# Weight stores and raw loads on GpSimd's queue, and the bonus' high part on GpSimd

## The chip, the cores and the metric

The kernel runs on one core of one Trainium2 chip. The metric is the time of one execution in device microseconds (us). The engines are named as in the profile: PE (TensorE, matrix products), DVE (VectorE), ACT (ScalarE), POOL (GpSimd) and SP (SyncE, which here only issues DMAs). DMAs can be issued by SP, ACT and POOL; each issue is an instruction in that engine's own stream, and an instruction that has to wait holds up all that stand behind it on its engine.

## The reference

One layer of a diffusion backbone over 128 context and 2048 latent tokens of 1024 channels. What matters here is the first part, up to the operands of the recurrence:

```python
h = _rmsnorm(x, norm_g) * (1 + scale) + shift          # scale, shift from c @ w_ada
proj = h @ w_in                                         # 1024 x 4096
r, k, v, g_a, b_gate, c_gate, u_conv, g_b = split(proj)
r, k, v = token_shift(r, k, v)                          # neighbours in the row
decay, a = low-rank maps of h (tanh / sigmoid), two directions
kk = k * kk_scale;  kk = kk * rsqrt(max(sum(kk * kk over a head), 1e-24))
kd = k * (1 + (a - 1) * ka_scale)                       # per direction
bonus = sum(r * kd * bonus_rk over a head, both directions)
y = groupnorm(scan(r, decay, kd, v, kk, a)) + bonus * v
```

Behind it come the bidirectional scan, the gates, the output projection with w_out, and a final norm.

## The kernel before, in words

All products are made in a split form: a float32 tensor is written as a high part in the matrix engine's format and a low part (the rest), and three products are summed: high by high, high by low, low by high. This holds for the weights and for the normalised input h, and for the small sums over a head, which are products with a matrix of ones.

The program has three phases, built by `phase1`, `phase2` and `phase3`. The change lies in `phase1`, which computes the projection and its followers. Tokens are cut into six blocks (`BLK`, five of 384 and one of 256), and two blocks form a third (`THIRD`). The outer loop runs over the thirds; within one, four groups `g` of 128 channels and two turns each (`turn`) load the weight blocks of 128 output channels that they need and run `mixA`, `gateA`, `convB` and `gateB` over the third's two token blocks.

- `load_w` (lines 117 to 129) gets a weight block. In the first third it is new: the raw block is loaded from `in_win` (line 124, tile `wr`, two buffers), ACT copies it into the high part (line 125), DVE subtracts for the low part (line 126, tile `w`, four buffers), and both parts are stored to the scratch tensor `scr_wsp` (line 127). In the second and third third the split block is loaded back from there (line 121).
- `parts_of` (lines 192 to 198) makes the parts of the summands of a head's sum: the high part `hsh` (line 196), the low part `hsl` (line 197). `part_sum` then runs two products with the ones (lines 204 and 205). It is called with names that begin with s for the squares of kk (`hshs`), with b for the bonus (`hshb`, from the tile `kd` that line 407 writes), and with q for the squares of a token block's norm (`hshq`).
- `shifted` (lines 313 to 330) copies a projection out of PSUM twice on ACT (lines 319 and 321), adds the neighbours on POOL (line 323, reading the padded tile `rawl`, two buffers) and joins both on DVE (line 329).
- `mixA` writes its results into tiles `sp` (four buffers) and spills them with SP (`spill`, line 335) to scratch tensors in memory, `scr_ops` among them; lines 387, 390, 398, 401 and 402 on DVE write these tiles.
- At the start the modulation is computed: `wadas` tiles are loaded (line 249), the rows are multiplied (line 190), copied (line 259), transposed (line 264), and made into scale and shift (lines 270 to 272). `norm_steps` squares a token block on ACT (lines 216 and 219), sums on DVE (line 220), and `make_h` makes h (lines 148 to 150). The first weight blocks, 32 and 33 (`wlora`), then 4 and 0 (`ws0`), are loaded in between, as are the token blocks x0 and x1 (line 177).

The order of the instructions on each engine isn't the order of the program text: a scheduler sets it when the program is built, from an estimate of each operation's duration. Changing one operation's engine can therefore move others.

Of the kernel before, what the change touches and what calls it, by code (L numbers as in the profile page):

```python
# [6 lines left out]
F32 = mybir.dt.float32  # L7
# [42 lines left out]
def phase1(K):  # L50
    nc, tc, A, S = K.nc, K.tc, K.A, K.S
    V, G, P, T = nc.vector, nc.gpsimd, nc.scalar, nc.tensor
# [64 lines left out]
    def load_w(cb):  # L117

        w = wp.tile([128, 2, 8, 128], F32R, tag="w", name=f"w{cb}_{K.u()}", bufs=4)
        if cb in kept:  # L120
            nc.sync.dma_start(w[:].bitcast(F32), S["wsp"][cb])
            return w
        raw = wp.tile([128, 8, 128], F32, tag="wr", name=f"wr{cb}_{K.u()}", bufs=2)
        nc.sync.dma_start(raw[:], A["win"][cb])
        P.copy(w[:, 0], raw[:])
        V.tensor_tensor(w[:, 1], raw[:], w[:, 0].bitcast(F32), ALU.subtract)
        nc.sync.dma_start(S["wsp"][cb], w[:].bitcast(F32))
        kept.add(cb)
        return w

# [61 lines left out]
    def parts_of(t_, n, nm, eng):  # L192

        hi = ta_.tile([128, 384], F32R, tag="hsh", name=f"hsh{nm}", bufs=1)
        lo = ta_.tile([128, 384], F32R, tag="vt", name=f"hsl{nm}", bufs=1)
        P.copy(hi[:, :n], t_[:, :n])  # L196
        eng.tensor_tensor(lo[:, :n], t_[:, :n], hi[:, :n].bitcast(F32), ALU.subtract)  # L197
        return hi, lo

    def part_sum(o, t_, n, nm, eng=G):  # L200

        hi, lo = parts_of(t_, n, nm, eng)
        ps = pax.tile([128, 384], F32, tag="ax", name=f"ps{nm}")
        T.matmul(ps[:, :n], o[:], hi[:, :n], start=True, stop=False)
        T.matmul(ps[:, :n], o[:], lo[:, :n], start=False, stop=True)
        return ps
# [38 lines left out]
    for i, b in enumerate((0, 2, 1, 3)):  # L245
# [7 lines left out]
        if i == 1:  # L253
            wlora = [load_w(32), load_w(33)]
            x1 = load_x(1, ca, "upx")
        if i == 2:
            ws0 = [load_w(cb) for cb in (4, 0)]
# [312 lines left out]

    for t3, js in enumerate(THIRD):
        wd, wi = wlora if t3 == 0 else (load_w(32), load_w(33))
        lws, pre, conv, sums = {}, {}, {}, {}
        more = coming(*THIRD[t3 + 1]) if t3 < 2 else iter(())
# [834 lines left out]
```

## Time and profile before

| | before |
|---|---|
| median of 3 runs | 1766.98 us (1766.21 to 1769.92) |
| profiled execution | 1765.65 us |
| its span, first to last instruction | 1763.5 us |
| mean granted clock of PE | 0.972 |
| DMA queue of SP (q1) | 323.99 MB, 61.5% of 16 engines' span |
| DMA queue of POOL (q0) | 4.46 MB, 0.7% |
| first raw load, last store of line 127 | issued at 7.1 and 358.6 us |
| phase 1's first third | up to about 400 us |

The profile shows one execution; its columns are explained where rows are shown. A line such as L124 is the line of the kernel's text. In the rows that group waits, the numbers are the total in us, the count, and the longest. In rows in order of time, the first number is the start in us, the second the duration, and the brackets hold how long the engine was idle just before and what released it.

### The profile page before, as it was taken

Reading aid. Unit: us, or ns where it says so; the run is one execution under the profiler, and the core shown is the slowest. Engines: PE = TensorE matmul, PEld = TensorE weight load, DVE = VectorE, ACT = ScalarE, POOL = GpSimd, SP = SyncE. Lnnn points to the kernel's source line nnn. Section 1 sums busy time; section 2 is a strip of 40 time slices with the busy share of each in tenths; the row PEclk is TensorE's granted clock in tenths of the full one; section 3 lists DMA queues with packets and bytes.
Section 4 is the critical chain, followed back from the end, with each engine's and each line's share of the span. In section 5 each row is a group of like instructions: output and inputs, shape, how many; then the busy total and the mean of one; then the engine's idle time right before and its main releaser. Section 6 shows DMA issues by size and latency. Waiting matters only on the chain. (4 is left out here: it accounts for less than half of the span.)

```text
span 1763.5 us, 33040 instructions
## 1 busy us (share of the span) xinstructions
PE 1638.5 (93%) x12400; PEld 1544.7 (88%) x12400; DVE 1163.8 (66%) x2249; ACT 815.3 (46%) x1583; POOL 585.4 (33%) x1089
## 2 busy tenths in 40 slices
PE   5999999998999998999999789899799899899998
PEld 2888889898999998999999789899799899887786
DVE  6875788866466866556773666677677777656333
ACT  4533455434144433334342367567577576533222
POOL 0011111101011111011120777767777868323221
PEclk8999999999999999999999899899999999899999
DMA  9787778785456646567767566667766875645442
GB/s 364 208 234 217 232 251 256 227 251 145 151 147 228 171 149 168 173 212 233 222 196 255 135 168 170 151 162 182 187 161 185 187 181 128 180 158 193 152 143 90
DMA packets 315664, 335.15 MB, mean 190 GB/s; under 512 B 166953, under 2 KB 263849, under 8 KB 301425
## 3 DMA queue, kind: packets, MB, share of 16 engines
q1 hardware_dynamic: 243200, 323.99, 61.5%
q10 hardware_dynamic: 70944, 4.60, 2.8%
q0 software_dynamic: 1360, 4.46, 0.7%
q8 instruction: 98, 1.61, 0.4%
q14 instruction: 62, 0.50, 0.1%
HBM read 221.16 MB, written 111.82 MB: 189 GB/s over the span
## 5 line engine op out<-in xcount | busy, mean ns | idle before, releaser
L934 POOL TENSOR_TENSOR zt<-zt,ztmp 128x30 f32<-128x30 f32 (+7 forms) x510 | 199.0, 390 | 39.1
L1010 PE MATMUL psE<-str,stl 128*128 128x128 f32 x1088 | 147.4, 280 | 13.0 <-DVE E L1011 11.1
L1050 PE MATMUL psS<-sv,E 128*128 128x64 f32 x1088 | 154.6, 274 | 2.0 <-DVE sv L1063 1.9
L1050 PEld LDWEIGHTS psS<-sv,E 128*128 128x128 f32 x1088 | 144.5, 198 | 5.2 <-DVE sv L1063 3.0
L1010 PEld LDWEIGHTS psE<-str,stl 128*128 128x128 f32 x1088 | 132.2, 193 | 15.4 <-DVE E L1011 12.0
L931 POOL TENSOR_TENSOR ztmp<-ab,zt 128x60 f32<-128x60 f32 (+7 forms) x255 | 133.1, 522 | 19.3
L779 ACT COPY bd<-rr 64x512 f32<-64x512 f32 x136 | 83.9, 617 | 84.1 <-issue 27.2
L323 POOL TENSOR_TENSOR shk<-rawl 128x384 f32<-128x384 f32 (+1 forms) x24 | 22.1, 920 | 292.3 <-ACT rawl L319 292.3
L1011 DVE TENSOR_TENSOR E<-psE,msk 128x512 f32<-128x512 f32 x136 | 93.2, 686 | 30.2 <-PE psE L1010 28.1
L1063 DVE TENSOR_TENSOR sv<-psS,pc 64x128 f32<-64x128 f32 x254 | 68.0, 277 | 42.1 <-PE psS L1050 40.4
L999 PE MATMUL psX<-F,zb 128*128 128x128 f32 x544 | 77.7, 295 | 18.5 <-DVE E L1011 17.1
L999 PEld LDWEIGHTS psX<-F,zb 128*128 128x128 f32 x544 | 70.5, 206 | 21.6 <-DVE E L1011 20.0
L892 PE MATMUL psF<-rr,bd 128*128 128x128 f32 x544 | 79.0, 291 | 9.9 <-DMA rr<-scr_ops 3.9
L1345 POOL TENSOR_TENSOR z<-z,x 128x512 f32<-128x512 f32 x32 | 43.6, 1366 | 129.1 <-DVE z L1341 107.1
L892 PE MATMUL psG<-rr,bd 128*128 128x128 f32 x544 | 73.9, 282 | 10.1 <-DVE F L893 10.1
L197 POOL TENSOR_TENSOR hslb<-kd,hshb 128x384 fp32r<-128x384 f32 (+1 forms) x24 | 26.0, 1084 | 163.7 <-ACT hshb L196 157.6
L892 PEld LDWEIGHTS psF<-rr,bd 128*128 128x128 f32 x544 | 70.3, 202 | 11.4 <-issue 6.1
L160 PE MATMUL mmc<-h,w 128*128 128x384 f32 (+1 forms) x192 | 67.5, 352 | 13.3 <-ACT q1r L321 9.7
L892 PEld LDWEIGHTS psG<-rr,bd 128*128 128x128 f32 x544 | 67.6, 196 | 10.4 <-DVE F L893 10.3
L323 POOL TENSOR_TENSOR shv<-rawl 128x384 f32<-128x384 f32 (+1 forms) x24 | 21.3, 888 | 151.9 <-ACT rawl L319 146.5
L893 DVE TENSOR_TENSOR F<-psF,msk 128x512 f32<-128x512 f32 x68 | 46.4, 683 | 30.4 <-PE psF L892 16.5
L162 PE MATMUL mmc<-h,w 128*128 128x384 f32 (+1 forms) x192 | 66.0, 344 | 0.0
(307 smaller groups left out, 5230.4 us busy)
## 6 DMA issues: line engine op xcount, KB each, us to landing
w<-scr_wsp SPq DMA_DIRECT2D x68, 1024.0 KB, 7.0
scr_wsp<-w SPq DMA_DIRECT2D x34, 1024.0 KB, 5.9
rr<-scr_ops SPq DMA_DIRECT2D x64, 512.0 KB, 4.8
scr_ops<-sp SPq DMA_DIRECT2D x160, 192.0 KB, 5.3
wr<-in_win SPq DMA_DIRECT2D x34, 512.0 KB, 6.3
ab<-scr_at SPq DMA_DIRECT2D x34, 256.0 KB, 4.1
x<-in_x SPq DMA_DIRECT2D x17, 512.0 KB, 3.8
wadas<-in_wada SPq DMA_DIRECT2D x8, 1024.0 KB, 13.0
```

What stands on the lines that cost most here:

```text
L160: T.matmul(ps[:, :n], w[:, 0, k], hh[:, 0, k, :n], start=k == 0, stop=False)
L162: T.matmul(ps[:, :n], w[:, 1, k], hh[:, 0, k, :n], start=False, stop=k == 7)
L779: (V.tensor_copy if k in ON_DVE else P.copy)(dst, src)
L892: T.matmul(ps[:, i, :].rearrange("p (a b) -> p a b", b=64), w[:, u, :], x[:, :, u, :], start=True, stop=True)
L893: V.tensor_tensor(dst[:, h * 4:h * 4 + 4, :], ps[:], mask.unsqueeze(1).broadcast_to((128, 4, 128)), ALU.mult)
L931: G.tensor_tensor(tv, ab[:, j:j + 2, j + 2:32].unsqueeze(1).broadcast_to((128, kn, 2, n)), zt[:, :kn, j:j + 2].unsqueeze(3).broadcast_to(( ...
L934: G.tensor_tensor(zt[:, :kn, j + 2:32], zt[:, :kn, j + 2:32], tv[:, :, r], ALU.subtract)
L999: T.matmul(px[:, i, :], B.zb[:, gi, us.start + i, :], g.F[:, us.start + i, :], start=True, stop=True)
L1010: T.matmul(pe[:, i, hd, :].rearrange("p (b t) -> p b t", b=2), g.lt[:, :, hd, us.start + k + i].rearrange("p b t -> p (b t)"), g.rt[:, :, ...
L1011: V.tensor_tensor(g.E[n][:, k:k + 2].rearrange("p a b c -> p (a b) c"), pe[:].rearrange("p a b c -> p (a b) c"), B.msk[:, ME[g.d]].unsquee ...
L1050: T.matmul(sp[gi][:, q, hd, :], g.E[n][:, k, hd, :], sv[:, u, hd, :], start=True, stop=True)
L1063: r = V.tensor_tensor(dst, sp[gi][0:64, q], B.pc[0:64, d, 2 * p:2 * p + 2, c:c + 1].broadcast_to((64, 2, 64)), ALU.mult)
```

## The change

Both DMAs of a new weight block, the raw load and the store of the parts, are issued by POOL instead of SP. And the high part of the bonus' summands (names that begin with b) is copied by POOL instead of ACT; the low part was POOL's already. The other sums' high parts stay on ACT. As each of the 34 weight blocks is new once, 34 loads and 34 stores move; 24 copies move, one for each group and token block, in all thirds.

```diff
         raw = wp.tile([128, 8, 128], F32, tag="wr", name=f"wr{cb}_{K.u()}", bufs=2)
-        nc.sync.dma_start(raw[:], A["win"][cb])
+        G.dma_start(raw[:], A["win"][cb])
         P.copy(w[:, 0], raw[:])
         V.tensor_tensor(w[:, 1], raw[:], w[:, 0].bitcast(F32), ALU.subtract)
-        nc.sync.dma_start(S["wsp"][cb], w[:].bitcast(F32))
+        G.dma_start(S["wsp"][cb], w[:].bitcast(F32))
...
         hi = ta_.tile([128, 384], F32R, tag="hsh", name=f"hsh{nm}", bufs=1)
         lo = ta_.tile([128, 384], F32R, tag="vt", name=f"hsl{nm}", bufs=1)
-        P.copy(hi[:, :n], t_[:, :n])
+        (G.tensor_copy if nm[0] == "b" else P.copy)(hi[:, :n], t_[:, :n])
         eng.tensor_tensor(lo[:, :n], t_[:, :n], hi[:, :n].bitcast(F32), ALU.subtract)
```

`G`, `V` and `P` are POOL, DVE and ACT.

## The prediction

> **What bounds the kernel now.** I read the busy times first, then a table of stretches, then the waits of each engine, then single rows in order of time.
>
> ```profile
> span 1763.5 us, 33040 instructions
> ```
>
> ```profile
> PE 1638.5 (93%) x12400; PEld 1544.7 (88%) x12400; DVE 1163.8 (66%) x2249; ACT 815.3 (46%) x1583; POOL 585.4 (33%) x1089
> ```
>
> TensorE (PE) is busy for 1638.5 of 1763.5 us, and only the 125 us that it is idle can be won; what makes it idle more is lost in full. The stretches say where that idle time lies (columns: busy time of PE, weight load, DVE, ACT, POOL, then granted clock, DMA share, GB/s).
>
> ```profile
> core 0: us, PE busy (x) PEld busy (x) DVE busy (x) ACT busy (x) POOL busy (x), PEclk, DMA share, GB/s
> 0.00:20.00 20.00, 7.64 (x40) 1.80 (x40) 6.07 (x23) 7.23 (x13) 1.27 (x15) 0.87 0.89 336
> 20.00:40.00 20.00, 15.50 (x84) 8.88 (x76) 16.62 (x36) 10.73 (x22) 0.00 (x0) 0.70 1.03 416
> 40.00:60.00 20.00, 15.64 (x71) 13.72 (x68) 19.39 (x42) 10.62 (x19) 0.00 (x0) 0.83 0.63 218
> ```
>
> ```profile
> 60.00:400.00 340.00, 321.76 (x1769) 305.29 (x1768) 253.88 (x449) 152.28 (x287) 44.37 (x42) 0.98 0.79 233
> 400.00:720.00 320.00, 304.22 (x1722) 299.76 (x1721) 202.90 (x365) 115.87 (x233) 40.81 (x42) 0.99 0.60 173
> ```
>
> There are three regimes. Up to 40 us the DMA engines are full (share 0.89 and 1.03, 336 and 416 GB/s): the start waits for data. From 40 to 60 us VectorE is full (19.39 of 20): it makes the normalised inputs. From 60 us on PE is the bound, with 340 - 321.76 = 18.2 us idle in the rest of the first third. The moved DMAs all lie before 360 us; the bonus edit reaches on to 910 us. The next rows are the waits in 60 to 400 us that the change touches (total, times, longest).
>
> ```profile
> SPq L127 <- DVE w L126: 72.4, 21, 12.1
> ```
>
> ```profile
> DVE sp L387 <- DMA scr_ops<-sp: 17.2, 6, 4.6
> ```
>
> ```profile
> ACT w L125 <- DMA wr<-in_win: 40.4, 14, 5.1
> ACT hshb L196 <- DVE kd L407: 21.1, 7, 6.3
> ```
>
> SyncE's queue stands for 72.4 us before weight stores whose data VectorE hasn't made. VectorE waits for operand spills, issued by the same queue, to land. ScalarE waits 40.4 us for raw weight blocks.
>
> **The change part by part.** It takes 34 stores of 1024 KB and 34 loads of 512 KB off SyncE's queue and puts them into GpSimd's instruction stream, and it moves 24 copies from ScalarE to GpSimd. In the built order the blocks keep their sequence; the start differs most, so it comes first.
>
> *Start.* Sizes and landings:
>
> ```profile
> scr_wsp<-w SPq DMA_DIRECT2D x34, 1024.0 KB, 5.9
> ```
>
> ```profile
> wr<-in_win SPq DMA_DIRECT2D x34, 512.0 KB, 6.3
> ```
>
> ```profile
> 8.47 0.43 SPq L177 DMA_DIRECT2D x<-in_xt  x1
> ```
>
> ```profile
> 22.89 0.33 SPq L127 DMA_DIRECT2D scr_wsp<-w  x1
> ```
>
> ```profile
> 25.65 0.52 ACT L216 ACTIVATE ssq<-x 128x384 f32<-128x384 f32 x1 [2.19 <-DMA x<-in_xt]
> ```
>
> ```profile
> 29.44 0.55 DVE L220 TENSOR_TENSOR ssq<-ssq,sqx 128x384 f32<-128x384 f32 x1
> ```
>
> ```profile
> 26.81 2.72 DVE L148 SCALAR_TENSOR_TENSOR x<-x,gs,ssq 128x128 f32<-128x128 f32 x8
> ```
>
> Before, one queue gives the order: the first two stores are issued at 22.89 us and later, behind the second input block x1 (issued 8.47 us) and the modulation weights. After, the first two raw loads are GpSimd's first DMAs, ScalarE's casts of them stand ahead of the squares of x0, and VectorE's two subtractions (L126) ahead of the sum of squares. So both stores and the next two raw loads are ready some 10 us after the start and travel beside x0 and x1: 2 x 1024 + 2 x 512 KB = 3.15 MB that weren't ahead of x1 before. At the mean of 336 and 416 GB/s they take 8.4 us. How two queues share the engines no row shows, so x1 lands between 0 and 8.4 us later than 25.65 us; I take the middle, 4.2 us. And the built order makes this bind: ScalarE now has four squares of x1 before the first h (L149), VectorE two of x1's sums before L148. Before, L148 began at 26.81 us, 1.16 us after x1; after, two squares (0.5 us each) and two sums lie between, about 2.0 us: +0.8, of which 1.1 us comes back because two sums of 0.55 us are then already made. With 19.39 of 20 us busy behind it, VectorE can't make the delay good, and at 60 us PE takes it over. Term: **+3.9 us** (ends -0.3 and +8.1). Nothing hides it; if the stores stayed behind x1, it would be nil.
>
> [...]
>
> *SyncE's queue freed.* Spills no longer stand behind the 72.4 us of store waits, nor on the same queue behind 1024 KB. VectorE's 17.2 us for spills shrink. What PE pays for that I take from PE's rows:
>
> ```profile
> 97.56 0.45 PE L365 MATMUL up<-lw,ups 128*128 128x384 f32 x1 [1.93 <-ACT q1r L321]
> 100.26 0.69 PE L160 MATMUL mmc<-h,w 128*128 128x384 f32 x1 [2.08 <-ACT ta L384]
> ```
>
> ```profile
> 159.80 0.44 PE L204 MATMUL pss<-hshs,onr 128*128 128x384 f32 x1 [2.38 <-ACT hshs L196]
> ```
>
> ```profile
> 182.98 0.44 PE L204 MATMUL pss<-hshs,onr 128*128 128x384 f32 x1 [1.77 <-ACT hshs L196]
> ```
>
> ```profile
> 264.56 0.44 PE L365 MATMUL up<-lw,ups 128*128 128x384 f32 x1 [1.30 <-ACT q1r L321]
> ```
>
> Followed back, the one at 182.98 us comes from a spill (1.8 us); the other four, 7.7 us, come from ScalarE standing at a late raw block, which the change doesn't cure: a load still follows its own store. Term: **-1.5 us** (0 to -1.8; the rivals take more).
>
> *GpSimd's stream.* The nearest rows for its DMAs are those of the second phase, a store of a quarter of the size.
>
> ```profile
> L935 POOL DMA_DIRECT2D scr_zt<-zt x17: 582/604/757, 1004.9 to 1519.4; - x17
> ```
>
> ```profile
> scr_zt<-zt POOLq DMA_DIRECT2D x17, 256.0 KB, 3.2
> ```
>
> An issue holds GpSimd for 0.60 us, and 3.2 us to landing is no more than the 5.9 of SyncE's larger stores. 68 x 0.60 = 41 us fit into the 296 us that GpSimd idles in 60 to 400 us. What counts is order: each store waits for VectorE's subtraction, and behind it are queued the shifted sums (VectorE waits for those) and the low parts (PE waits). The times that each operation has now, set against the new order, show what that costs. Of 42 operations one stands behind a DMA that is due later:
>
> ```profile
> 183.00 1.30 POOL L197 TENSOR_TENSOR hsls<-sq,hshs 128x384 fp32r<-128x384 f32 x1 [6.23 <-ACT hshs L196]
> ```
>
> ```profile
> 186.57 0.43 SPq L124 DMA_DIRECT2D wr<-in_win  x1
> ```
>
> That is 3.6 us on one low part. The other way round, six raw loads now stand behind operations that end 0.4 to 2.5 us after the load's present issue, 8.8 us together; the first and the last pair:
>
> ```profile
> 83.99 1.42 POOL L197 TENSOR_TENSOR hsls<-sq,hshs 128x384 fp32r<-128x384 f32 x1 [17.85 <-ACT hshs L196]
> ```
>
> ```profile
> 85.00 0.39 SPq L124 DMA_DIRECT2D wr<-in_win  x1
> ```
>
> ```profile
> 303.32 0.83 POOL L323 TENSOR_TENSOR shv<-rawl 128x384 f32<-128x384 f32 x1
> ```
>
> ```profile
> 302.88 0.42 SPq L124 DMA_DIRECT2D wr<-in_win  x1
> ```
>
> PE paid 7.7 us for ScalarE's 40.4, a fifth; a fifth of 8.8 is 1.7 us. Term: **+1.5 us** (0 to 3.6 + 1.7 = 5.3).
>
> [...]
>
> *The bonus' high part.* ScalarE's copy goes, GpSimd gets one of the same size.
>
> ```profile
> L196 ACT CAST hshb<-kd x24: 406/513/517, 87.0 to 908.0; 128x384 fp32r<-128x384 f32 x20, 128x256 fp32r<-128x256 f32 x4
> ```
>
> ```profile
> L197 POOL TENSOR_TENSOR hslb<-kd,hshb 128x384 fp32r<-128x384 f32 x20 | 23.1, 1153 | 145.5 <-ACT hshb L196 139.3 <-PE pss L205 6.2
> ```
>
> GpSimd's copy isn't in the trace; it has one input where the subtraction has two, so it lies between ScalarE's 0.51 and the subtraction's 1.15 us: 0 to 0.64 us later per sum. ScalarE no longer stands at kd (21.1 us in the first third), but PE waits little for what is behind it. Where PE does wait for this part, kd itself is late, and that stays:
>
> ```profile
> 688.77 0.44 PE L204 MATMUL psb<-hshb,onr 128*128 128x384 f32 x1 [3.25 <-ACT hshb L196]
> ```
>
> Gain at most those 3.25 us; loss at most 24 x 0.64 x a fifth = 3.1 us. Term: **+0.1 us**.
>
> Sum: 3.9 - 1.5 + 1.5 + 0.1 = +4.0 us. Its own ends are -0.3 - 1.8 + 0 - 3.2 = -5.3 and 8.1 + 0 + 5.3 + 3.1 = +16.5. The profiled execution took 1765.65 us (2.15 around its span), 1.3 below the median of 1766.98, so it becomes 1769.7, and a median **1771.0 us**. This case's ends are 1762 and 1783.
>
> **The rivals.** First, faster: the start costs nothing, because the stores come too late to matter or SyncE's transfers hold their share, and freeing the queue wins more than one PE wait, also raw blocks that land sooner. Of the 18.2 us PE idle, the five rows hold 9.5; with two thirds gone, -6.3, so 1760.7 us. For it: 72.4 us of waits leave SyncE. Against: loads keep their place behind stores, and PE is 94% busy there. It decides if x1 lands before about 26 us. Second, no change: the start costs +1.5 and the queue gives it back, 1767 us. Third, slower on a larger scale: each time a raw block is late, GpSimd stands at its store until VectorE's subtraction (1.22 us in the next row) and two issues are done, 2.4 us longer than ScalarE stands. At all 14 late blocks that is 34 us, a fifth of it on PE 6.8; with the start at its upper end, 8.1 + 6.8 = +15, so 1782 us. Against: only one of 42 operations stood behind a later DMA. It decides if low parts wait over 1 us at most stores.
>
> ```profile
> L126 DVE TENSOR_TENSOR w<-wr,w x34: 1162/1219/1641, 21.6 to 357.3; 128x1024 fp32r<-128x1024 f32 x34
> ```
>
> [...] That the edit does nothing is excluded: the built order shows all 68 DMAs and 24 copies moved.
>
> The later phases are also reordered a little on PE; I see no sign in it and count it only in the range.
>
> **How the numbers follow.** Forecast (slower by about 4 us) 0.37, first rival 0.27, second 0.20, third 0.12, fourth 0.04. A measurement of this kernel tells about 0.2%, 3.5 us, from no change. The forecast's case reaches from a little below its bound to +12; of its 0.37 some 0.04 falls inside 0.2%, while the second rival gives 0.03 to either side. Slower 0.33 + 0.16 + 0.03 = 0.52, same 0.04 + 0.14 = 0.18, faster 0.27 + 0.03 = 0.30. The range takes the first rival's figure with a few us below it and the third's: 1758 to 1786 us. The forecast's own range is 1762 to 1783.
>
> **What would show it.** Right: the first square of x1 (L216) some 4 us later than 25.65, L148 near 31, PE's first shifted operands near 68; GpSimd's issues near 0.60 us; VectorE's wait for spills before 400 us well under 17.2; PE's waits for the bonus' parts as before. [...]

## The result and the profile after

The changed kernel takes 1779.21 us in the median of 11 runs (1771.36 to 1785.17); the kernel before, run beside it, takes 1767.36 us (1763.94 to 1769.92). The ratio is 1.0061, 95% interval 1.0043 to 1.0078: slower by 10.8 us (7.6 to 13.8). The profiled execution of the changed kernel took 1784.01 us. Its page begins:

```profile
span 1782.2 us, 33110 instructions
...
PE 1641.3 (92%) x12400; PEld 1548.9 (87%) x12400; DVE 1164.4 (65%) x2249; ACT 804.0 (45%) x1559; POOL 638.6 (36%) x1181
```

PE does the same work (1641.3 us against 1638.5) and idles for 140.9 us where it idled for 125.0. The stretches, columns as before:

```profile
0.00:20.00 20.00, 5.74 (x24) 2.21 (x24) 4.67 (x18) 5.08 (x6) 4.67 (x21) 1.00 0.88 318
20.00:40.00 20.00, 8.59 (x36) 3.59 (x40) 12.26 (x28) 10.23 (x24) 0.00 (x0) 1.00 1.03 419
```

```profile
60.00:400.00 340.00, 316.71 (x1706) 297.62 (x1705) 260.99 (x461) 152.99 (x288) 83.37 (x108) 0.96 0.78 224
```

Up to 40 us the DMA engines are as full as before (318 and 419 GB/s), but PE gets 14.33 us of work done instead of 23.14, and VectorE 16.93 instead of 22.69: the engines carry bytes that nobody waits for yet. From 60 to 400 us PE idles for 23.3 us instead of 18.2. The rows that answer to the predicted first steps, from the order of time on ACT and DVE:

```profile
33.74 0.52 ACT L216 ACTIVATE ssq<-x 128x384 f32<-128x384 f32 x1 [0.90 <-DMA x<-in_xt]
```

```profile
36.58 2.71 DVE L148 SCALAR_TENSOR_TENSOR x<-x,gs,ssq 128x128 f32<-128x128 f32 x8
```

x1's first square is 8.1 us later (25.65 before) and L148 9.8 us later (26.81 before). The waits of 60 to 400 us (total, times, longest):

```profile
POOL scr_wsp L127 <- DVE w L126: 68.2, 14, 10.1
ACT w L125 <- DMA wr<-in_win: 39.0, 14, 6.8
...
POOL hshb L196 <- DVE kd L407: 24.9, 5, 9.2
...
DVE sp L387 <- DMA scr_ops<-sp: 15.2, 4, 5.0
```

The 72.4 us for which SP stood at the stores until VectorE's low part was made are now POOL's 68.2; ScalarE waits for raw blocks as long as before (39.0 against 40.4), and VectorE for spills nearly as long (15.2 against 17.2).

### The profile page after: what moved, and what is told of

The parts are those of the page before. It is cut to its first block, busy times and chain, and to the rows that moved or that the text cites. A ratio compares the mean times of both kernels' runs of the same rounds, so it can differ in the third digit from the quotient of the medians.

```text
span 1782.2 us, 33110 instructions
## 1 busy us (share of the span) xinstructions
PE 1641.3 (92%) x12400; PEld 1548.9 (87%) x12400; DVE 1164.4 (65%) x2249; ACT 804.0 (45%) x1559; POOL 638.6 (36%) x1181
## 5 line engine op out<-in xcount | busy, mean ns | idle before, releaser
L160 PE MATMUL mmc<-h,w 128*128 128x384 f32 (+1 forms) x192 | 68.5, 357 | 16.9 <-ACT q1r L321 14.5
L127 POOL DMA_DIRECT2D scr_wsp<-w x34 | 19.0, 560 | 143.0 <-DVE w L126 83.5
L161 PE MATMUL mmc<-h,w 128*128 128x384 f32 (+1 forms) x192 | 67.0, 349 | 0.0
L162 PE MATMUL mmc<-h,w 128*128 128x384 f32 (+1 forms) x192 | 66.7, 348 | 0.0
```

The costliest lines, as they stand in the source:

```text
L160: T.matmul(ps[:, :n], w[:, 0, k], hh[:, 0, k, :n], start=k == 0, stop=False)
L161: T.matmul(ps[:, :n], w[:, 0, k], hh[:, 1, k, :n], start=False, stop=False)
L162: T.matmul(ps[:, :n], w[:, 1, k], hh[:, 0, k, :n], start=False, stop=k == 7)
```

## The experiments

I held two theories when I began. **Start**: the first four blocks' DMAs take the DMA engines from what the start needs, and that delay stays to the end. **Stream**: from the fifth block on, loads and stores in one stream on GpSimd come late for each other. The rival was **Bonus**, the copy itself, on which the expectations of e3 and e4 put a price of its own.

These runs were made on three chips, on which the kernel before took 1774 to 1775 us in the median, so versions are compared by their ratio to the runs of before beside them. The table also holds two places of each profile: L148, and the start of the first product (`mml`) of the second third, which sums up the first third. In the profiles they read, for before and after:

```profile
390.08 0.33 PE L160 MATMUL mml<-h,w 128*128 128x384 f32 x1
```

```profile
407.28 0.33 PE L160 MATMUL mml<-h,w 128*128 128x384 f32 x1
```

| version | L148 | second third | ratio to before (95%) | us |
|---|---|---|---|---|
| before; again | 26.81; 26.73 | 390.1; 391.5 | 1 | |
| the change; again | 36.58; 36.38 | 407.3; 405.8 | 1.0061 (1.0043 to 1.0078); 1.0068 (1.0042 to 1.0093) | +10.8; +12.1 |
| e1: first four blocks on SP | 26.64 | 403.4 | 1.0053 (1.0034 to 1.0072) | +9.4 |
| e2: first four blocks alone on GpSimd | 36.69 | 407.6 | 1.0107 (1.0079 to 1.0135) | +19.0 |
| e3: all DMAs, no bonus copy | 36.54 | 405.6 | 1.0022 (1.0000 to 1.0045) | +3.9 |
| e4: bonus copy alone | 26.75 | 395.4 | 1.0026 (1.0002 to 1.0050) | +4.6 |
| e7: later stores alone | 26.90 | 393.4 | 0.9991 (0.9971 to 1.0011) | -1.6 |
| e8: later loads alone | 27.05 | 394.4 | 1.0006 (0.9991 to 1.0022) | +1.1 |
| e9: later loads and stores | 26.74 | 397.7 | 1.0059 (1.0037 to 1.0082) | +10.5 |
| e10: first four blocks on ScalarE's queue | 43.77 | 411.7 | 1.0090 (1.0068 to 1.0113) | +16.0 |
| e11: x1 loaded first | 26.78 | 394.5 | 0.9999 (0.9985 to 1.0014) | -0.2 |
| e12: x1 first, later stores | 27.48 | 396.1 | 1.0005 (0.9990 to 1.0021) | +0.9 |

The us are the ratio's distance from 1 times the median of before in the same set of runs (1774.83 for e1 to e4, 1774.03 for e7, e8 and the second run of the change, 1773.91 for e9 to e12).

**e1, e2: the start put back, and the start alone.**

```diff
-        G.dma_start(raw[:], A["win"][cb])
+        (nc.sync if cb in (32, 33, 4, 0) else G).dma_start(raw[:], A["win"][cb])
...
-        G.dma_start(S["wsp"][cb], w[:].bitcast(F32))
+        (nc.sync if cb in (32, 33, 4, 0) else G).dma_start(S["wsp"][cb], w[:].bitcast(F32))
```

That is e1, against the changed kernel. e2 has `G` and `nc.sync` the other way round in both lines, and the bonus' copy on ScalarE.

> The changed kernel, but the first four weight blocks (32, 33, 4, 0) are loaded and stored by SyncE's queue again; the other thirty and the bonus' copy stay with GpSimd. Theory Start (the stores and raw loads of these four travel beside x0, the modulation weights and x1, and the 9.8 us by which the first shift comes later stay to the end): x1's first square near 26 us, the first shift near 27, and the time about 10 us below the changed kernel's 1779, so 1768 to 1771. Theory Stream (GpSimd stands at the later stores and loads, or its adds come behind them; PE loses another 5 us between 60 and 400 us): the start is as before, but the time stays 5 us or more above before's 1767, so 1772 to 1776, and PE is idle for about 23 us between 60 and 400 us as in the changed kernel.

> The kernel before, with the loads and stores of the first four weight blocks alone (32, 33, 4, 0) on GpSimd's queue; everything else on SyncE's and ScalarE's as before. Theory Start: x1's first square near 33 us, the first shift near 36, PE's work from there on 9 to 10 us later, the time about 10 us above before's, 1776 to 1778. Theory Stream: the later blocks are needed for the loss; the start's delay is partly made up before 60 us and the time is 1767 to 1772.

In e1 the start is as before to 0.2 us, and the loss stays: +9.4 us. Start alone is not the cause. In e2 L148 is 9.9 us late, as in the changed kernel, and the whole version is slower by 14 to 24 us. Start is enough to make the kernel slower, and by more than its 10 us; at the second third e2 is as late as the change (407.6 against 407.3 and 405.8).

In e1 PE runs level with before up to 110 us and then falls back by several us, first at one place. In order of time, on GpSimd, ScalarE and PE:

```profile
114.98 0.58 POOL L127 DMA_DIRECT2D scr_wsp<-w  x1 [6.23 <-DVE w L126]
115.56 0.53 POOL L124 DMA_DIRECT2D wr<-in_win  x1
```

```profile
126.83 1.04 ACT L125 CAST w<-wr 128x1024 fp32r<-128x1024 f32 x1 [10.36 <-DMA wr<-in_win]
```

```profile
127.93 0.69 PE L160 MATMUL mmb<-h,w 128*128 128x384 f32 x1 [4.49 <-ACT w L125]
```

The raw load is issued 0.58 us behind a store for which GpSimd stood until VectorE's low part was made, and its 512 KB need 11.3 us to land; the store's 1024 KB, in the same queue ahead, need 10.0. ScalarE idles for 10.36 us, PE for 4.49. Why both take so long comes with e8 and e9.

**e3, e4: the bonus.** e3 puts line 196 back to `P.copy`; e4 is before with the changed line 196 alone.

> The changed kernel with the bonus' high part copied by ScalarE again; all DMAs of the first third's blocks stay with GpSimd. Theories Start and Stream: nothing much changes, 1777 to 1782, within 3 us of the changed kernel. Theory Bonus (GpSimd's copy stands behind a store's wait, or takes GpSimd's time in the later thirds, where the changed kernel's PE falls back by another 6 us between 720 and 1080 us): 4 to 8 us under the changed kernel.

> The kernel before, with the bonus' high part alone copied by GpSimd; all DMAs on SyncE's queue. Theories Start and Stream: within 2 us of before, 1765 to 1769. Theory Bonus: 3 us or more above before, 1770 to 1775.

Both came out as the rival Bonus had it: alone the copy costs 4.6 us (0.4 to 8.9), and with it the DMAs cost 7 us more than without (e3 against the change). Yet by the time of the whole it adds nothing to the later DMAs (e1 against e9), though at the second third e1 is 5.7 us behind e9. The contrasts disagree, and no row here shows what the copy would cost. So Bonus is neither shown nor excluded; nothing to 9 us is what the runs leave.

**Again: two executions of one program.**

> The kernel before, unchanged, for a second profile: how far do two executions of one program differ? If times and places are made by the instructions' order, every stall of over 1 us between 60 and 400 us comes back at its place, x1's first square is near 25.6 us, PE's idle time there is 18 us within 1.5, and the span moves only with the granted clock. If they are chance, stalls of several us come at other places.

> The changed kernel, unchanged, on the same chip and beside the same runs of before as the part kernels. Theory Start (its 10 us stay to the end): about 10 us above before. Theory Start and Stream: the two add up, 15 to 19 us above before. If the two cover each other (blocks that are late wait for nobody when PE is late as well): 5 to 10 us, no more than the start alone or the later blocks alone.

The stalls come back at their places. Before: 2.38 us at 159.80 and 2.20 at 159.01, 1.77 at 182.98 and 2.00 at 182.33. After: 4.21 at 191.88 and 4.78 at 192.14. The change came out at +12.1 us here (7.5 to 16.5), between mere cover (5 to 10) and the full sum (15 to 19), and its interval touches both. Up to 700 us two executions agree to about 3 us. Behind that they part: the first product of phase 2 (`psF`) came at 939.3 us and at 948.6 us in two executions of before. So profiles are read here up to the second third, and ends by the ratios alone.

**e7, e8, e9: later stores, later loads, both.** Each is the kernel before with the first four blocks on SP and the bonus on ScalarE; e7 puts line 127 on `G` from the fifth block on, e8 line 124, e9 both.

> The kernel before, with the stores alone on GpSimd's queue, from the fifth block on; all loads and the first four blocks stay with SyncE. Theory Stream (a raw load stands behind the store of the block before it on GpSimd, which waits for VectorE's low part): no load stands there, so within 2 us of before, or up to 3 us faster since SyncE is freed. If stores on GpSimd hold up its adds: 4 us or more above before, and PE waits for the shifted sums or low parts.

> The kernel before, with the raw loads alone on GpSimd's queue, from the fifth block on; all stores and the first four blocks stay with SyncE. Theory Stream: a load stands no longer behind a store, only behind GpSimd's adds and subtractions, so the wait of 4.5 us near 128 us for the ScalarE copy of a late block is gone and the time is within 3 us of before. If GpSimd's own work is enough to make loads late: that wait is there, 3 us or more, and the time is 5 to 9 us above before.

> The kernel before, with loads and stores of all blocks from the fifth on on GpSimd's queue; the first four blocks stay with SyncE, the bonus' copy with ScalarE. Stores alone and loads alone cost nothing that could be measured, so theory Stream (it takes both, since only then a load stands behind the store of the block before it) says: a wait of 3 to 5 us for the ScalarE copy of a late block near 128 us, PE 7 to 13 us later than before from 130 us on, and a time 5 to 9 us above before. If the loss of the version with the bonus' copy came from that copy: no such wait, and within 3 us of before.

Neither alone costs anything that can be measured; both together cost 10.5 us (6.6 to 14.5). That is Stream, without bonus and without the start, though not quite as I expected it: the time is above the 5 to 9 us, and PE's wait near 128 us is 2.34 us instead of 3 to 5. The same block in e8 and in e9:

```profile
113.25 0.53 POOL L124 DMA_DIRECT2D wr<-in_win  x1 [12.06 <-DVE w L126]
```

```profile
120.71 1.07 ACT L125 CAST w<-wr 128x1024 fp32r<-128x1024 f32 x1
```

```profile
115.24 0.58 POOL L127 DMA_DIRECT2D scr_wsp<-w  x1 [5.02 <-DVE w L126]
115.82 0.53 POOL L124 DMA_DIRECT2D wr<-in_win  x1
```

```profile
125.59 1.04 ACT L125 CAST w<-wr 128x1024 fp32r<-128x1024 f32 x1 [5.72 <-DMA wr<-in_win]
126.69 0.44 PE L160 MATMUL mmb<-h,w 128*128 128x384 f32 x1 [2.34 <-ACT w L125]
```

In e8 (first two fences) the load, too, waits for VectorE, which frees its raw buffer, but no store goes ahead of it in its queue: it lands 6.4 us on, and ScalarE doesn't wait. In e9 it is issued 2.6 us later, behind the store, and lands 9.8 us on.

The store's bytes ahead are only a part of that. Stretches of e9 and then of e8 (DMA share and GB/s are the last two columns):

```profile
116.00:122.00 6.00, 6.00 (x35) 5.66 (x34) 6.00 (x8) 1.43 (x4) 2.62 (x4) 1.00 0.99 135
122.00:128.00 6.00, 2.96 (x16) 2.33 (x14) 2.23 (x5) 2.19 (x4) 0.00 (x0) 1.00 0.94 388
```

```profile
112.00:119.00 7.00, 7.00 (x41) 6.76 (x39) 7.00 (x11) 3.52 (x6) 1.56 (x2) 1.00 0.90 309
120.00:126.00 6.00, 6.00 (x34) 5.91 (x35) 6.00 (x7) 2.81 (x7) 1.90 (x2) 1.00 1.04 111
```

Each has 6 us in which the DMA engines are full by their packets' times and move a third of what they move beside it. In both this follows a small transfer that ScalarE issues, `scr_pc` (line 392): 784 packets, 0.003 MB, which start at 115.3 us in e9 and at 119.4 in e8, and in e1 at 115.1, with 130 GB/s from 116 to 122 us. In e9 and e1 the store and the load fall into this stretch; in e8 the load has landed before it, at 119.6 us. So the late block has two candidates, the store ahead in the queue and the small transfer ahead of both, and no run parts them. This is one place. Another is common to e1, e9, e3 and both profiles of the change; e9's rows, on DVE, ACT and PE:

```profile
184.74 0.56 DVE L387 TENSOR_TENSOR sp<-kk,pp 128x384 f32<-128x384 f32 x1 [5.26 <-DMA scr_ops<-sp]
```

```profile
187.37 0.48 ACT L319 COPY rawl<-mmr 128x384 f32<-128x384 f32 x1 [6.08 <-DVE ob L464]
```

```profile
188.39 0.69 PE L160 MATMUL mmc<-h,w 128*128 128x384 f32 x1 [4.25 <-ACT q1r L321]
```

VectorE stands for 5.26 us at a spill's buffer (3.50 us at this place before); behind it is the work that frees `rawl`, ScalarE waits for that, and PE for ScalarE. Before, the built order had ScalarE copy this product later, behind other work, and PE paid 0.41 us there and 1.77 us just before. So part of Stream is the order that the scheduler made from the moved DMAs; no run parts it from the queue.

**e10: another queue for the start.** As e2, with `nc.scalar` in place of `G`.

> [...] Theory Start (any second queue whose transfers are issued early takes its share of the DMA engines from x0, the modulation weights and x1): x1's first square near 33 us and the first shift near 36, as with GpSimd's queue, and a time 10 us or more above before. [...]

It is no cheaper: +16.0 us (12.1 to 20.0) against e2's +19.0 (14 to 24), so the loss comes with ScalarE's queue too. The rows of PE:

```profile
22.67 1.94 PE L190 MATMUL psrow<-wadas,scp 128*32 128x512 f32 x8 [6.05 <-DMA wadas<-in_wada]
38.13 0.69 PE L204 MATMUL psq<-hshq,onf 128*128 128x384 f32 x1 [11.44 <-ACT hshq L196]
```

```profile
31.65 0.34 ACTq L124 DMA_DIRECT2D wr<-in_win  x1
32.03 0.52 ACT L216 ACTIVATE ssq<-x 128x384 f32<-128x384 f32 x1 [23.89 <-DMA x<-in_xt]
```

The modulation weights are late here as well (16.63 us before), so ScalarE's queue takes engine time from them as well (2.48 MB and 28.1% of the engines from 8 to 29 us), 6 us here where GpSimd's took 9 to 10. And ScalarE itself, standing at its fourth raw load until 31.65 us, reaches x0's squares only then; how much of the 16 us is its own standing, no run parts. My expectation for x1 (33 us) missed that: it is 39.93.

**e11, e12: the start from its other side.**

```diff
+            x1 = load_x(1, ca, "upx")
             wlora = [load_w(32), load_w(33)]
-            x1 = load_x(1, ca, "upx")
```

> The kernel before, all DMAs on SyncE's and ScalarE's queues, with one thing moved: x1 is loaded ahead of the raw blocks 32 and 33 instead of behind them. Theory Start from its other side (the landing of x1 sets the first shift): 1 MB less ahead of x1, at the 420 GB/s that the transfers before 40 us ran at 2.5 us, so x1's first square near 23 us, the first shift near 24, the first product near 25.5 instead of 28.15, and a time 2 to 4 us below before, unless the raw blocks, 3.5 us later, hold up the first product in turn (they were copied at 20.23 and 22.43, so ready at 23.5; shifted they are ready at 27): then the gain is 1 us or less.

> The same, x1 ahead of the raw blocks 32 and 33, with the stores from the fifth block on on GpSimd's queue, which alone came out at 0.9991 of before. Theories Start and Stream: the sum of the two, 2 to 6 us below before, faster than both kernels of this study.

x1's first square came at 23.15 us, 2.5 us sooner as expected, and L148 at 26.78 us against 26.81: x1 does not set it. e11 is no faster, and e12 neither; no version of this study beats the kernel before by a measurable amount. What sets L148 stands in PE's rows, of before and of the changed kernel:

```profile
16.63 1.94 PE L190 MATMUL psrow<-wadas,scp 128*32 128x512 f32 x8 [3.00 <-DMA wadas<-in_wada]
19.04 1.94 PE L190 MATMUL psrow<-wadas,scp 128*32 128x512 f32 x8 [0.47 <-DMA wadas<-in_wada]
20.90 0.69 PE L204 MATMUL psq<-hshq,onf 128*128 128x384 f32 x1
```

```profile
25.55 1.93 PE L190 MATMUL psrow<-wadas,scp 128*32 128x512 f32 x8 [8.10 <-DMA wadas<-in_wada]
29.35 1.94 PE L190 MATMUL psrow<-wadas,scp 128*32 128x512 f32 x8 [1.86 <-DMA wadas<-in_wada]
31.21 0.69 PE L204 MATMUL psq<-hshq,onf 128*128 128x384 f32 x1
```

The second pair of modulation weights lands 8.9 and 10.3 us later. x0's sum of squares (L204) stands behind them in PE's order and is 10.3 us later; its square root, the reciprocals and L148 follow. The wait for x1 in the changed kernel runs beside that chain.

## Why the prediction was right or wrong

**Sign and size.** Slower was the likeliest sign and 1779.21 lies in the range and in the forecast's own range; the forecast's +4.0 was too small by 7 us. Two terms were mis-sized, and in the larger one the gate behind the delay was named wrongly, so that the sign came out right for a chain that is only in part the one forecast.

**Start: +3.9 forecast.** The step that failed is "x1 lands between 0 and 8.4 us later [...]; I take the middle", and with it the chain behind: the gate was named wrongly. x1 came 8.1 us later, near the bound of 8.4. How the queues share the engines shows in the traffic of 8 to 29 us of the changed kernel (packets, MB, share of the engines):

```profile
q1 hardware_dynamic: 1573, 4.97, 64.2%
q0 software_dynamic: 599, 3.20, 36.4%
```

GpSimd's queue moved 3.20 MB there, so the 3.15 MB that I had counted did travel ahead of x1's first square at 33.74 us; how the two queues share the engines beyond that, these rows don't show. SP's queue alone moved 8.58 MB in the same time before. The upper end of +8.1 was the better figure. But the chain led through the modulation weights, which I had named only as something ahead of the stores; x1's squares and sums, on which I spent the working, don't set L148 (e11). L148 came 9.8 us later, past my upper end of 8.1. That VectorE can't make it good was right: the second third starts 16.1 us late in e2, against before's second profile (407.6 and 391.5), so the delay even grew by 6 us. It didn't grow by waits. From the first `mml` product to the second third, in before and in e2:

```profile
47.50:390.10 342.60, 322.61 (x1756) 305.24 (x1756) 261.92 (x468) 157.96 (x299) 44.37 (x42) 0.98 0.78 231
```

```profile
59.30:407.60 348.30, 328.09 (x1755) 309.62 (x1755) 260.63 (x467) 157.99 (x298) 45.27 (x43) 0.96 0.78 227
```

PE idles for 20.0 and 20.2 us; the 5.5 us lie in its busy time over the same products, at a granted clock of 0.96 instead of 0.98. The last section comes back to that clock.

**SyncE's queue freed: -1.5 forecast.** Not seen. SP's 72.4 us at the stores went, but in their place SP stands longer at the spills themselves, whose data VectorE has yet to make (all 60 to 400 us, before and after):

```profile
SPq L335 <- DVE sp L387: 50.0, 14, 11.4
```

```profile
SPq L335 <- DVE sp L387: 99.0, 14, 16.6
```

So most of the spills were not late for standing behind stores. e7, which frees SP of the later stores, measured -1.6 us (-5.1 to +2.0): a gain of that size can't be excluded.

**GpSimd's stream: +1.5 forecast, end +5.3.** e9 measured +10.5 (6.6 to 14.5) for it without the start. The failed step is to set the times of before against the new order: it took each operation's time as given, so it saw 0.4 to 2.5 us per load. It didn't see that the store's 1024 KB then travel ahead of the load's 512 KB in the one queue, and both behind ScalarE's small transfer (9.8 and 11.3 us to landing in e9 and e1), nor that VectorE's subtraction on which both hang moved in the built order, from 106.56 us before to 113.74 in e9. Which of these makes the 10.5 us stays open. The third rival named the right wait, GpSimd at a store whose block is late; PE waited once for such a block's copy (1.8 us), not 14 times. Issue times were right: 0.60 us forecast, 0.57 and 0.53 in the median here and 0.705 at most (min, median, max in ns). The fourth rival, at a chance of 0.04, counted on issues that are held up; these rows show none:

```profile
L127 POOL DMA_DIRECT2D scr_wsp<-w x34: 531/569/626, 8.1 to 379.7; - x34
```

```profile
L124 POOL DMA_DIRECT2D wr<-in_win x34: 527/530/705, 1.3 to 366.5; - x34
```

**The bonus' part: +0.1 forecast, -3.25 to +3.1.** GpSimd's copy takes 0.60 us in the median (bounds 0.51 and 1.15); e4's +4.6 (0.4 to 8.9) overlaps the end, and so does the 7 us between the change and e3. Not settled.

**Why the whole is less than its parts.** Against before's second profile the second third is late by 16.1 us from the start alone, 6.2 from the later DMAs, 3.9 from the bonus, together 26; the change shows 14.3 and 15.8. When PE is late by 10 us, a late block finds it waiting less: the wait for ScalarE's copy is 4.49 us at 127.93 in e1 and 1.83 us in the changed kernel:

```profile
134.74 0.44 PE L160 MATMUL mmb<-h,w 128*128 128x384 f32 x1 [1.83 <-ACT w L125]
```

**What stays open.** e2 is slower than e3, which contains it, by more than their intervals allow for chance, though at the second third they differ by 2 us. The rest arises behind 700 us, where each version has its own order and where two executions of one program already part by several us. e3 also contains e9, and is 6.6 us faster than it. So the end time of one version can be off the worth of its part by some 7 to 15 us, and the end times are not sums of parts; the delays up to the second third are the firmer ground. There the start alone makes the whole delay of the change, and the later DMAs and the bonus add nothing to it that shows. Reordering in the later phases was in my range and not in a term; no run isolates it.

## What to carry to other kernels

A second DMA queue was a second place in line here, not only a second issuer: with the first four blocks on it, PE had the modulation weights 8.9 and 10.3 us later in the changed kernel and 6.0 us later in e10 (22.67 against 16.63). So before moving early transfers to another queue, list what the start waits for and ask which of it now shares the engines, beginning with the last operand of the chain that gates, found by following the gate back through every engine's order. And a load that was moved together with the store of the block before it into one stream stood behind that store, for which GpSimd waited 5.02 us in e9, and landed 9.8 us on, where the load moved alone landed 6.4 us on (e8); moved apart, each cost nothing here that could be measured (-1.6 and +1.1 us). Look also at what else is under way when it travels: a transfer of 0.003 MB stood before the 6 us of e9 in which all queues together moved 135 GB/s, against 388 in the next 6. With a built order, set the new order's own times against each other, not the old ones.

## What the runs showed of the hardware that was not expected

A wait of PE of 4 us or more cost more than its length in these runs. In the changed kernel, products that follow each other:

```profile
187.33 0.34 PE L205 MATMUL psb<-hslb,onr 128*128 128x384 f32 x1
191.88 0.65 PE L160 MATMUL mmc<-h,w 128*128 128x384 f32 x1 [4.21 <-ACT q1r L321]
192.33 0.52 PE L161 MATMUL mmc<-h,w 128*128 128x384 f32 x1
...
195.64 0.34 PE L160 MATMUL mmc<-h,w 128*128 128x384 f32 x1
195.82 0.33 PE L161 MATMUL mmc<-h,w 128*128 128x384 f32 x1
```

```profile
191.88:195.20 3.32, 3.32 (x10) 3.32 (x11) 3.32 (x7) 3.32 (x7) 2.71 (x3) 0.51 0.20 81
195.20:199.00 3.80, 3.80 (x23) 3.80 (x23) 3.73 (x6) 3.69 (x8) 2.29 (x3) 0.98 1.00 323
```

After the wait of 4.21 us they start 0.32 us apart instead of 0.17 until 195.2 us, and the granted clock (the column behind POOL) is 0.51: 1.6 us lost again. In the fourteen profiles here all 25 waits of PE of 4 us or more between 70 and 720 us were followed by such a stretch at a clock of 0.50 or 0.51, which went on for 3.3 to 6.5 us; that is worth 1.6 to 3 us each, by an estimate from the two spacings. Shorter waits differ: behind the 3.25 us before 688.77 us in the kernel before, the clock is 1.00 for 8 us; behind the 2.08 us before 100.26 us it is 0.50 for 3.0 us, and in e2, behind the 1.98 us before 137.93 us, it is 0.51 from there to 141.3 us. I put e2's 5.5 us down to such stretches, for its one wait of 4 us or more comes behind the second third, at 449.94 us. The prediction priced waits at their length. What lowers the clock and what brings it back, no run here shows.
